# A hybrid S5 and SSD layer: the SSD chain in another order of steps, and C A^j formed a second time instead of stored and loaded

## The chip, the core and the metric

The kernel runs on one core of one Trainium2 chip. Its engines work side by side, each in its own order: TensorE (PE; its weight loads are PEld) multiplies, VectorE (DVE), ScalarE (ACT) and GpSimd (POOL) do elementwise work, and SyncE (SP) issues every DMA of this kernel, one after the other. The metric is the device time of one execution in microseconds; before is the median of three runs.

## What is computed

One layer over 1024 frames of 1024 features: a projection of the normed input feeds two branches, whose outputs are joined by W_out; a gated per-layer input and a last norm follow. The two branches that the change touches, cut to the core:

```python
def s5_branch(u, ...):             # 64 groups of 16 channels, 64 complex states each
    states = A_bar * states_before + u @ B_bar          # per step, a scan
    y = real(states @ C) + D * u
    y = gelu(y); return y * sigmoid(y @ w_glu + b_glu)

def ssd_chunked(xs, dt, A, Bm, Cm):                     # 16 heads, 4 B/C groups, state 128
    xd = xs * dt
    scores = (C @ B.T) * exp(segsum(dt * A))            # decays within a chunk
    y_diag = scores @ xd
    states = B.T @ (decay * xd);  y_off = (C @ states_before) * exp(cumsum(dt * A))
    return y_diag + y_off
```

## The kernel before

A float32 matmul is done as three fast ones: each operand is split in a high and a low part (`whi`, `wlo` from the loaded weights `wraw`), and a dense tile (L163) is 48 matmuls of 512 columns. 56 such tiles run one after the other and make up most of the time: 8 for u, 20 for the convolution and some z (SEQ names them, c or z), 12 more for z, 8 for GLU and 8 for the joint output. In between, generators for the S5 and the SSD branch are moved forward by `pull(gen, n)`, which runs n steps of them; the tables PU, PX, PZ, PG and PO say how many steps follow each tile. The order in which a step is written is only a start: the program is then put in order by a scheduler that simulates time, so an edit in one place can move instructions elsewhere. Each engine runs its own instructions strictly in that order.

S5, with b the eighth of the 64 groups:

- s5_weights (L346 to L399), in the first conv tiles: per b it loads `br` (one buffer, L367) and `gr`, forms `wx` from them (L373 to L376) and the product `CA` = C A^j for nine powers j on VectorE (L386 to L391), stores CA to DRAM as `CAd` (L393), and one b later `strips` multiplies B by CA (L353) and stores the result as `Kd`. `in_line` keeps the strips' matmuls behind the product L374.
- s5_states: loads `ug` (two buffers, L404) and multiplies two b at a time (L428). Then a scan over the states on VectorE (L444, L445).
- s5_out: per b it takes `CAr`, `tp` (cut out of Kd by 8 loads, L473) and ug, all with two buffers and loaded one b ahead (L470), multiplies (L487, L488), applies Gelu on ACT into the buffer of tp, and stores that as `Yd` (L491).

SSD runs over eight k, each 128 frames. Per k: `load` of `cc` (L583) and of `csB` (L586, 1 MB, one row for each head spread over 128 partitions), two buffers each; 16 decays on VectorE (L601) and an exponential on ACT; scores on TensorE (L608), multiplied into csB (L610); xs transposed (L617) and multiplied by dt to `xd` (L621); y on TensorE (L633) with its additions (L635), and from k = 1 on the part from the state (L641, `E0B`); a gate (L648), a norm (L175 to L178, L666) and a store `Sd` (L667); the next state `st` (L675, L680, L682).

## Time and profile before

| | us |
|---|---|
| median of the runs (1004.63 to 1007.05) | 1006.27 |
| the profiled execution | 1008.08 |
| its span, from first to last instruction | 1006.3 |
| PE busy | 964.5 |
| DVE busy | 596.1 |
| ACT busy | 453.3 |
| POOL busy | 215.7 |

The rows of the trace that matter stand in the section on rows. In them L163 is line 163 of the kernel, `out<-in` are the tiles written and read, a number in square brackets is how long the engine stood idle before the instruction and what ended that, and PEclk is the granted clock of TensorE as a share of 2.4 GHz (0.50 is its level of 1.2 GHz).

### The profile page before, as it was taken

The numbers are of one execution on the slowest core, as the hardware profiler recorded it, in microseconds if no ns is written. First come the engines' busy times: TensorE is split into PE (matmuls) and PEld (weight loads), VectorE is DVE, ScalarE is ACT, GpSimd is POOL, SyncE is SP. The second block draws the span as 40 slices with busy tenths as digits, with TensorE's granted clock in tenths as the row PEclk, the third lists the DMA queues.
The fourth block names the chain that finished last, engine by engine and source line by source line (L and its number), as shares of the span: only waits on it lengthen the run. The fifth ranks groups of instructions, "written<-read, shape, count | busy, mean of one in ns | idle before, by whom it ended". The sixth has DMA issues, their size and how long they took to land. (4 is left out here: it accounts for less than half of the span.)

```text
span 1006.3 us, 12839 instructions
## 1 busy us (share of the span) xinstructions
PE 964.5 (96%) x4902; PEld 802.5 (80%) x4902; DVE 596.1 (59%) x959; ACT 453.3 (45%) x583; POOL 215.7 (21%) x150
## 2 busy tenths in 40 slices
PE   9999979997999999989989999899999999999995
PEld 5788857786888888778778888787788888888994
DVE  6599688953988994000656878678611611444436
ACT  7444122354855544224455844557233431463235
POOL 0000000000000043001123445454341284242000
PEclk9999989998999999999989999999999999999998
DMA  7135777568423125997996877465455341010004
GB/s 296 38 88 144 201 221 259 179 191 205 137 94 105 64 105 187 257 261 215 246 310 181 241 188 217 142 168 174 137 167 168 99 128 41 1 67 1 2 1 168
DMA packets 133965, 153.31 MB, mean 152 GB/s; under 512 B 6032, under 2 KB 107408, under 8 KB 132880
## 3 DMA queue, kind: packets, MB, share of 16 engines
q1 hardware_dynamic: 133904, 152.49, 52.0%
q8 instruction: 39, 0.64, 0.3%
q14 instruction: 22, 0.18, 0.1%
HBM read 112.82 MB, written 39.65 MB: 152 GB/s over the span
## 5 line engine op out<-in xcount | busy, mean ns | idle before, releaser
L163 PE MATMUL psd<-xnlo,whi 128*128 128x512 f32 x592 | 185.7, 393 | 0.0
L163 PE MATMUL psd<-xnhi,whi 128*128 128x512 f32 x592 | 185.4, 393 | 0.0
L163 PE MATMUL psd<-xnhi,wlo 128*128 128x512 f32 x592 | 184.3, 392 | 0.2 <-DVE wlo L142 0.2
L139 ACT ACTIVATE whi<-wraw 128x1024 fp32r<-128x1024 f32 x71 | 74.8, 1056 | 217.2 <-PE psd L163 184.7
L142 POOL TENSOR_TENSOR wlo<-wraw,whi 128x1024 fp32r<-128x1024 f32 x44 | 119.2, 2712 | 247.2 <-ACT whi L139 235.8
L163 PEld LDWEIGHTS psd<-xnlo,whi 128*128 128x128 f32 x592 | 110.8, 189 | 24.7 <-issue 1.6
L163 PEld LDWEIGHTS psd<-xnhi,wlo 128*128 128x128 f32 x592 | 110.8, 188 | 24.2 <-issue 1.0
L163 PEld LDWEIGHTS psd<-xnhi,whi 128*128 128x128 f32 x592 | 111.0, 189 | 23.1 <-issue 0.4
L601 DVE SCALAR_TENSOR_TENSOR csB<-csB,csM,cst_t 128x128 f32<-128x128 f32 x128 | 45.9, 432 | 101.3 <-DMA m<-Yd 94.0
L574 DVE SCALAR_TENSOR_TENSOR cv<-pad,prm_t,cv 128x1024 f32<-128x1024 f32 x48 | 65.7, 1369 | 12.1 <-ACT cv L572 11.9
L565 POOL MEMSET pad<- 128x3 f32 x16 | 1.6, 103 | 215.8 <-DMA Cd<-pad 169.6
L892 DVE TENSOR_TENSOR h<-h,psd 128x512 f32<-128x512 f32 x16 | 10.4, 684 | 63.3 <-PE psd L163 63.3
L163 PE MATMUL psd<-hhi,wlo 128*128 128x384 f32 (+2 forms) x168 | 46.9, 340 | 0.0
L163 PE MATMUL psd<-hlo,whi 128*128 128x384 f32 (+2 forms) x168 | 46.7, 338 | 0.0
L163 PE MATMUL psd<-hhi,whi 128*128 128x384 f32 (+2 forms) x168 | 46.5, 338 | 0.0
L933 DVE TENSOR_TENSOR gt<-psd,rstdB 128x384 f32<-128x384 f32 (+2 forms) x21 | 11.1, 559 | 52.3 <-PE psd L163 42.3
L142 DVE TENSOR_TENSOR wlo<-wraw,whi 128x1024 fp32r<-128x1024 f32 x27 | 32.9, 1220 | 14.3 <-ACT whi L139 14.3
L163 PE MATMUL psd<-yhi,whi 128*128 128x512 f32 x128 | 41.0, 398 | 0.0
L163 PE MATMUL psd<-yhi,wlo 128*128 128x512 f32 x128 | 40.7, 395 | 0.0
L163 PE MATMUL psd<-mhi,wlo 128*128 128x512 f32 x128 | 40.0, 391 | 0.0
L163 PE MATMUL psd<-ylo,whi 128*128 128x512 f32 x128 | 40.0, 391 | 0.0
L163 PE MATMUL psd<-mlo,whi 128*128 128x512 f32 x128 | 39.5, 390 | 0.0
(292 smaller groups left out, 1878.0 us busy)
## 6 DMA issues: line engine op xcount, KB each, us to landing
wraw<-in_w_in_dram SPq DMA_DIRECT2D x39, 512.0 KB, 3.7
Cd<-pad SPq DMA_DIRECT2D x16, 512.0 KB, 3.1
Zd<-z SPq DMA_DIRECT2D x16, 512.0 KB, 3.8
ug<-Ud SPq DMA_DIRECT2D x16, 512.0 KB, 6.6
cc<-Cd SPq DMA_DIRECT2D x8, 1024.0 KB, 9.0
csB<-Rd SPq DMA_DIRECT2D x8, 1024.0 KB
wraw<-in_w_out_dram SPq DMA_DIRECT2D x16, 512.0 KB, 4.3
CAd<-CA SPq DMA_DIRECT2D x16, 288.0 KB, 4.6
```

The source lines that it names most:

```text
L139: S.activation(hi, raw, AF.Copy)
L142: E.tensor_tensor(lo, raw, f(hi), ALU.subtract)
L163: T.matmul(p, w[:, c], rhs[k][r][:, x], start=(k == 0 and j == 0), stop=(k == nk - 1 and j == 2))
L565: G.memset(pad[:, 8:11, 0:1], 0.0)
L574: conv_last[0] = V.scalar_tensor_tensor(cv, pad[:, d:d + 8, 1:129], pr("convw", 4 * m + d), cv, ALU.mult, ALU.add)
L601: i_ = V.scalar_tensor_tensor(csB[:, h], csB[:, h], csM[:, 16 * k + h:16 * k + h + 1], cap, ALU.subtract, ALU.min)
L892: V.tensor_tensor(hf(h_t[m], h), hf(h_t[m], h), ps[h], ALU.add)
L933: first = V.tensor_tensor(gt, pg[i], rstdB[:, c], ALU.mult)
```

## The change

S5's weights. CA has eight powers instead of nine, its store CAd goes, the strips are no longer held behind L374, and the first two entries of PX are 1 and 5 instead of 3 and 3.

```diff
-PX = [3, 3, 1, 1, 2, 1, 2, 1, 0, 2, 1, 2, 2, 0, 1, 1, 2, 2, 2, 2]
+PX = [1, 5, 1, 1, 2, 1, 2, 1, 0, 2, 1, 2, 2, 0, 1, 1, 2, 2, 2, 2]
...
-            def strips(b, CA, behind):
+            def strips(b, CA):
                 kp = psa()
                 for q in range(4):
                     for ri in range(2):
-                        i_ = T.matmul(kp[32 * q:32 * q + 32, 0:P], Bbd[:, ri, 4 * b + q, :],
-                                      CA[:, ri, q, 0:8, :].rearrange("p a b -> p (a b)"),
-                                      start=(ri == 0), stop=(ri == 1), tile_position=(0, 32 * q))
-                        in_line((behind, i_))
+                        T.matmul(kp[32 * q:32 * q + 32, 0:P], Bbd[:, ri, 4 * b + q, :],
+                                 CA[:, ri, q].rearrange("p a b -> p (a b)"),
+                                 start=(ri == 0), stop=(ri == 1), tile_position=(0, 32 * q))
...
-                behind = V.tensor_tensor(w1, br, gr[:, 1:2].broadcast_to([P, 2, 512]), ALU.mult)
+                V.tensor_tensor(w1, br, gr[:, 1:2].broadcast_to([P, 2, 512]), ALU.mult)
...
-                CA = q2.tile([P, 2, 4, 9, 16], F32, tag="CA", name="CA")
-                ca1 = q2.tile([P, 4, 9, 16], F32, tag="ca1", name="ca1", bufs=1)
+                CA = q2.tile([P, 2, 4, 8, 16], F32, tag="CA", name="CA")
+                ca1 = q2.tile([P, 4, 8, 16], F32, tag="ca1", name="ca1", bufs=1)
...
-                er = Er[:, J0:J0 + 9, g4].rearrange("p j g -> p g j")[:, :, :, None].broadcast_to(sh)
+                er = Er[:, J0:J0 + 8, g4].rearrange("p j g -> p g j")[:, :, :, None].broadcast_to(sh)
...
-                for g2 in range(2):
-                    dma(CAd[b, g2].rearrange("r n c -> n r c"),
-                        CA[64 * g2:64 * g2 + 64].rearrange("p a b c d -> p a (b c d)"))
                 if b > 0:
-                    strips(b - 1, last, behind)
+                    strips(b - 1, last)
                 last = CA
                 yield
-            strips(7, last, behind)
+            strips(7, last)
```

S5's output. CAr is not loaded; a new input `crow` holds C with the states along the rows, of which `cb` (128 KB) is loaded for each b. `EO` holds the powers, copied once by ACT in eight pieces of 64x256. `rows(b)` forms C A^j again in three VectorE operations of 128x1024, one b ahead. The old body of s5_out did the same matmuls with CAr in place of CA.

```diff
     def load_out(q4, b):
-        CA = q4.tile([P, 2, 4, 144], F32, tag="CAr", name="CAr")
-        dma(CA.rearrange("p a b c -> p a (b c)"), CAd[b].rearrange("g r n c -> (r n) g c"))
+        cb = q4.tile([P, 2, 8, 16], F32, tag="cb", name="cb")
+        dma(cb, crow[:, b])
         tp = q4.tile([P, 8, P], F32, tag="tp", name="tp")
         for s in range(8):
             dma(tp[16 * s:16 * s + 16],
                 Kd[b].rearrange("(g h) c -> h g c", h=16)[:, :, 112 - 16 * s:240 - 16 * s])
-        return CA, tp, load_u(q4, b)
...
+        return cb, tp, load_u(q4, b)
+
+    def s5_out(Er, Ei, wx, q4, ahead):
+        with tc.tile_pool(name="q5", bufs=1, side="right") as q5:
+
+            EO = q5.tile([P, 2, 8, 64], F32, tag="EO", name="EO")
+            lo_, up = slice(0, 64), slice(64, P)
+            for g2, src in enumerate((lo_, up)):
+                for r, j, x, sign in ((lo_, 0, Er, 1.0), (lo_, 1, Ei, 1.0), (up, 0, Ei, -1.0), (up, 1, Er, 1.0)):
+                    S.activation(EO[r, j, :, g2:64:2], x[src, J0 + 1:J0 + 9], AF.Copy, scale=sign)
+
+            def rows(b, cb):
+
+                CA = q5.tile([P, 8, 8, 16], F32, tag="CAo", name="CAo", bufs=2)
+                t = q5.tile([P, 8, 8, 16], F32, tag="cat", name="cat")
+                for j, dst in ((0, CA), (1, t)):
+                    V.tensor_tensor(dst, cb[:, j, :, None, :].broadcast_to([P, 8, 8, 16]),
+                                    EO[:, j, :, 8 * b:8 * b + 8].rearrange("p j g -> p g j")[:, :, :, None].broadcast_to([P, 8, 8, 16]),
+                                    ALU.mult)
+                V.tensor_tensor(CA.rearrange("p g j c -> p (g j c)"), CA.rearrange("p g j c -> p (g j c)"),
+                                t.rearrange("p g j c -> p (g j c)"), ALU.subtract)
+                return CA
+            CA = rows(0, ahead[0][0])
             yield
+            for b in range(8):
+                _, tp, ug = ahead.pop(0)
+                if b < 7:
+                    ahead.append(load_out(q4, b + 1))
+                    nxt = rows(b + 1, ahead[0][0])
+                ysb = tp.rearrange("p (q g) c -> p q g c", g=2)
+                for g2 in range(2):
+                    yp = psa()
+                    for q in range(4):
+                        o = yp[:, q * P:(q + 1) * P]
+                        g = 2 * q + g2
+                        T.matmul(o, tp[:, g, :], ug[:, g, :], start=True, stop=False)
+                        T.matmul(o, CA[:, g].rearrange("p j c -> p (j c)"), wx[:, 8 * b + g].rearrange("p r c -> p (r c)"), start=False, stop=True)
+
+                    S.activation(ysb[:, :, g2, :].rearrange("p q (s j) -> p q s j", j=8), js(yp), AF.Gelu_apprx_tanh)
+                dma(Yd[8 * b:8 * b + 8].rearrange("g t h c -> (t h) g c"), tp)
+                CA = nxt
+                yield
```

SSD. csB is loaded ahead of cc and both two k ahead; the decays of k + 1 are made in two halves in iteration k, its scores and the load E0B at the end of iteration k; two more steps are pulled before the loop.

```diff
                 cc = p4.tile([P, 16, P], F32, tag="cc", name="cc", bufs=2)
-                dma(cc, Cd[:, :, k * P:(k + 1) * P].rearrange("m p c -> p m c"))
                 csB = p4.tile([P, 16, P], F32, tag="csB", name="csB", bufs=2)
                 src = Rd[0, 16 * k:16 * k + 16, :].rearrange("h l -> (h l)")
                 dma(csB.rearrange("p h l -> p (h l)"), src[None].broadcast_to([P, 2048]))
+                dma(cc, Cd[:, :, k * P:(k + 1) * P].rearrange("m p c -> p m c"))
                 return cc, csB
...
+            def load_e(k):
+
+                E0B = p4.tile([P, 8, P], F32, tag="E0B", name="E0B", bufs=1)
+                for hh in range(2):
+                    dma(E0B[64 * hh:64 * hh + 64], Rd[1, 16 * k + hh:16 * k + 16:2, :][None].broadcast_to([64, 8, P]))
+                return E0B
+
+            def decays(k, csB, half):
+                for h in range(8 * half, 8 * half + 8):
                     i_ = V.scalar_tensor_tensor(csB[:, h], csB[:, h], csM[:, 16 * k + h:16 * k + h + 1], cap,
-                                           ALU.subtract, ALU.min)
+                                                ALU.subtract, ALU.min)
                     if k == 0:
                         in_line((conv_last[0], i_))
-                S.activation(csB, csB, AF.Exp)
+                if half:
+                    S.activation(csB, csB, AF.Exp)
+
+            def scores(cc, csB):
                 sp = psa()
                 for g in range(4):
                     T.matmul(sp[:, g * P:(g + 1) * P], cc[:, 8 + g], cc[:, 12 + g], start=True, stop=True)
                 for g in range(4):
                     V.tensor_tensor(csB[:, 4 * g:4 * g + 4], csB[:, 4 * g:4 * g + 4],
                                     sp[:, None, g * P:(g + 1) * P].broadcast_to([P, 4, P]), ALU.mult)
+
+            st = None
+            cur, nxt = load(0), load(1)
+            yield
+            for half in range(2):
+                decays(0, cur[1], half)
+            yield
+            scores(*cur)
+            yield
+            for k in range(8):
+                cc, csB = cur
+                zc = p4.tile([P, 8, P], F32, tag="zc", name="zc")
+                dma(zc, Zd[8:16, :, k * P:(k + 1) * P].rearrange("m p c -> p m c"))
                 xd = p4.tile([P, 16, 64], F32, tag="xd", name="xd")
                 xd2 = p4.tile([P, 16, 64], F32, tag="xd2", name="xd2") if k < 7 else None
...
                 yield
-                if k < 7:
-                    nxt = load(k + 1)
...
+                if k < 7:
+                    decays(k + 1, nxt[1], 0)
                 yield
...
+                    decays(k + 1, nxt[1], 1)
                 yield
...
                     st = st2
+                    E0B = load_e(k + 1)
+                    scores(*nxt)
+                    cur = nxt
+                    nxt = load(k + 2) if k < 6 else None
                 yield
...
+    cn = lambda c: c.transpose(2, 0, 1).reshape(64, 8, 8, 16)
+    a["crow"] = np.ascontiguousarray(np.tile(np.stack([cn(one["s5_C_re"]), cn(one["s5_C_im"])], 2), (2, 1, 1, 1, 1)))
```

Line numbers of the new program differ: there L371, L372 and L374 are the wx of before, L384 to L389 make CA, L468 loads tp, L486 and L489 are `rows`, L509 stores Yd, L618 are decays, L630 scores, L654 xd, L666 the additions to ys, L681 the gate, L700 the norm's product and L716 copies of st.

On VectorE, in the strips of b = 1 and 2, before (ca_851 and ca_852 are the halves of CA(2), which the third group of strips reads):

```order
L388 TENSOR_TENSOR CA<-ca_851,ca_852 128x576
L373 TENSOR_TENSOR wx<-br,gr 128x1024
L374 TENSOR_TENSOR w_843<-br,gr 128x1024
L389 TENSOR_TENSOR ca_851<-csb,Ei 128x576
L390 TENSOR_TENSOR ca_852<-csb,Er 128x576
L142 TENSOR_TENSOR wlo<-wraw,whi 128x1024
L376 TENSOR_TENSOR wx<-wx,w_843 128x8x64 x2
L574 SCALAR_TENSOR_TENSOR cv<-pad,prm_t,cv 128x1024
L391 SCALAR_TENSOR_TENSOR CA<-ca_851,ca_852 128x576
```

and now, where ca_846 and ca_847 are those halves:

```order
L386 TENSOR_TENSOR CA<-ca_846,ca_847 128x512
L357 SCALAR_TENSOR_TENSOR Ks<-cst_t,prm_t,psa 128x16
L358 COPY Ks<-psa 128x112
L374 TENSOR_TENSOR wx<-wx,w_806 128x8x64 x2
L387 TENSOR_TENSOR ca_846<-csb,Ei 128x512
L388 TENSOR_TENSOR ca_847<-csb,Er 128x512
L371 TENSOR_TENSOR wx<-br,gr 128x1024
L372 TENSOR_TENSOR w_838<-br,gr 128x1024
L389 SCALAR_TENSOR_TENSOR CA<-ca_846,ca_847 128x512
```

The last operation of CA(2) stood behind wlo, two sums of wx and a conv step (L574), and now stands right behind the products wx.

On SP, in the output stage, from the load of ug(3) on, before:

```order
L404 DMA ug<-Ud 128x8x128
L470 DMA CAr<-CAd 128x2x576
L491 DMA Yd<-tp 128x8x128
L473 DMA tp<-Kd 16x8x128 x8
L808 DMA Zd<-z 128x1024
L473 DMA tp<-Kd 16x8x128 x8
L138 DMA wraw<-in_w_in_dram 128x1024
L404 DMA ug<-Ud 128x8x128
L470 DMA CAr<-CAd 128x2x576
L491 DMA Yd<-tp 128x8x128
L404 DMA ug<-Ud 128x8x128
```

and now, from the store of b = 1 on:

```order
L509 DMA Yd<-tp 128x8x128
L468 DMA tp<-Kd 16x8x128 x16
L465 DMA cb<-in_crow_dram 128x256
L846 DMA Zd<-z 128x1024
L137 DMA wraw<-in_w_in_dram 128x1024
L399 DMA ug<-Ud 128x8x128
L509 DMA Yd<-tp 128x8x128
L465 DMA cb<-in_crow_dram 128x256
L399 DMA ug<-Ud 128x8x128
L468 DMA tp<-Kd 16x8x128 x8
L509 DMA Yd<-tp 128x8x128
```

Before, the stores of b = 2 and 3 were both issued ahead of the loads of tp(4); now the loads of tp(4), eight of them, stand between Yd(2) and Yd(3), and so on for the following b.

On VectorE, in SSD, from the scores of k = 0 on (xd_3875 belongs to k = 1), before:

```order
L610 TENSOR_TENSOR csB<-csB,psa 128x512 x4
L601 SCALAR_TENSOR_TENSOR csB<-csB,csM,cst_t 128x128 x16
L635 SCALAR_TENSOR_TENSOR ys<-cc,prm_t,psa 128x128 x8
L648 TENSOR_TENSOR ys<-ys,zc 128x1024
L176 TENSOR_TENSOR nl<-zc,nh 128x512
L682 COPY st<-psa 128x512 x2
L666 TENSOR_TENSOR ys<-ys,zc 128x1024
L610 TENSOR_TENSOR csB<-csB,psa 128x512 x4
L601 SCALAR_TENSOR_TENSOR csB<-csB,csM,cst_t 128x128 x11
L621 TENSOR_TENSOR xd<-psa,dt_76 128x512
L621 TENSOR_TENSOR xd_3875<-psa,dtd 128x512
```

and now, from the decays of k = 0 on:

```order
L618 SCALAR_TENSOR_TENSOR csB<-csB,csM,cst_t 128x128 x32
L630 TENSOR_TENSOR csB<-csB,psa 128x512 x4
L654 TENSOR_TENSOR xd<-psa,dt_76 128x512
L654 TENSOR_TENSOR xd_3745<-psa,dtd 128x512
L654 TENSOR_TENSOR xd<-psa,dt_76 128x512
L654 TENSOR_TENSOR xd_3745<-psa,dtd 128x512
L666 SCALAR_TENSOR_TENSOR ys<-cc,prm_t,psa 128x128 x8
L681 TENSOR_TENSOR ys<-ys,zc 128x1024
L175 TENSOR_TENSOR nl<-zc,nh 128x512
L618 SCALAR_TENSOR_TENSOR csB<-csB,csM,cst_t 128x128 x16
L716 COPY st<-psa 128x512
L700 TENSOR_TENSOR ys<-ys,zc 128x1024
```

32 decays, those of k = 0 and 1, now stand ahead of the scores of k = 0, and the 16 decays of k = 2 ahead of the copies of st, the norm's product and, behind those, the scores (L630) and xd of k = 1; before, 11 decays of k = 2 stood behind the scores of k = 1 and ahead of its xd.

## Rows read from the trace of the kernel before

**Rows 1.** Page, busy us (share of the span) and number of instructions of each engine.

```profile
PE 964.5 (96%) x4902; PEld 802.5 (80%) x4902; DVE 596.1 (59%) x959; ACT 453.3 (45%) x583; POOL 215.7 (21%) x150
```

**Rows 2.** Waits of TensorE: tile, line, for what: us in total, times, longest.

```profile
PE psa L353 <- DVE CA L391: 7.5, 1, 7.5
PE psa L428 <- DMA ug<-Ud: 5.5, 1, 5.5
PE psa L487 <- DMA tp<-Kd: 5.2, 3, 2.8
...
PE psa L617 <- ACT zc L663: 2.1, 1, 2.1
```

**Rows 3.** Timeline of TensorE, SSD's y: start us, us, ..., xcount, [idle before <-releaser].

```profile
489.90 3.21 PE L633 MATMUL psa<-csB,xd 128*64 128x128 f32 x32 [1.72 <-DVE csB L610]
...
523.20 1.97 PE L633 MATMUL psa<-csB,xd 128*64 128x128 f32 x16 [3.59 <-DVE xd L621]
```

**Rows 4.** Stretches behind two waits: engines' busy us (xinstructions), then PEclk, DMA share, GB/s.

```profile
142.70:146.10 3.40, 3.40 (x20) 2.52 (x21) 3.40 (x5) 0.00 (x0) 0.00 (x0) 0.50 1.01 284
...
519.61:528.90 9.29, 5.70 (x40) 4.93 (x40) 8.36 (x25) 3.23 (x3) 1.01 (x2) 0.63 1.00 337
```

**Rows 5.** Timeline of TensorE, dense matmuls ahead of the strips' wait.

```profile
129.91 0.61 PE L163 MATMUL psd<-xnhi,whi 128*128 128x512 f32 x2
...
131.72 0.62 PE L163 MATMUL psd<-xnlo,whi 128*128 128x512 f32 x2
```

**Rows 6.** Timeline of VectorE, the products wx and the last operation of CA(2).

```profile
124.89 1.23 DVE L373 TENSOR_TENSOR wx<-br,gr 128x1024 f32<-128x1024 f32 x1 [1.87 <-DMA br<-in_brow_dram]
...
134.71 1.23 DVE L373 TENSOR_TENSOR wx<-br,gr 128x1024 f32<-128x1024 f32 x1 [3.93 <-DMA br<-in_brow_dram]
...
141.86 0.75 DVE L391 SCALAR_TENSOR_TENSOR CA<-ca,ca 128x576 f32<-128x576 f32 x1
```

**Rows 7.** Timeline of SP, issues of br in the strips.

```profile
118.70 0.38 SPq L367 DMA_DIRECT2D br<-in_brow_dram  x1
...
127.28 0.39 SPq L367 DMA_DIRECT2D br<-in_brow_dram  x1
```

**Rows 8.** Timeline of SP, issues of ug in the states (the first with ug(1)).

```profile
213.67 2.09 SPq L404 DMA_DIRECT2D ug<-Ud  x2
...
226.98 0.38 SPq L404 DMA_DIRECT2D ug<-Ud  x1
```

**Rows 9.** Stretch of the output stage, columns as in rows 4.

```profile
395.00:476.00 81.00, 75.85 (x424) 66.14 (x423) 0.00 (x0) 27.04 (x35) 11.96 (x5) 0.98 0.89 247
```

**Rows 10.** Instructions of tile wlo on POOL: ns min/median/max, first and last start us.

```profile
L142 POOL TENSOR_TENSOR wlo<-wraw,whi x44: 2360/2402/7515, 360.9 to 922.7; 128x1024 fp32r<-128x1024 f32 x44
```

**Rows 11.** Timeline of SP, store of b = 0 and loads of b = 2 and 3.

```profile
392.68 0.68 SPq L491 DMA_DIRECT2D Yd<-tp  x1
...
401.21 5.67 SPq L473 DMA_DIRECT2D tp<-Kd  x8
```

**Rows 12.** Timeline of TensorE, first and last output matmuls.

```profile
388.54 0.39 PE L488 MATMUL psa<-wx,CAr 128*128 128x128 f32 x2
...
463.19 0.39 PE L488 MATMUL psa<-wx,CAr 128*128 128x128 f32 x2
```

**Rows 13.** Timeline of SP, loads csB of k = 1 and k = 2.

```profile
480.64 4.30 SPq L586 DMA_DIRECT2D csB<-Rd  x1
...
509.97 0.74 SPq L586 DMA_DIRECT2D csB<-Rd  x1
```

**Rows 14.** Timeline of VectorE in SSD, k = 0 and 1.

```profile
493.31 4.29 DVE L601 SCALAR_TENSOR_TENSOR csB<-csB,csM,cst_t 128x128 f32<-128x128 f32 x16 [1.68 <-DMA csB<-Rd]
...
513.59 2.48 DVE L610 TENSOR_TENSOR csB<-csB,psa 128x512 f32<-128x512 f32 x4
518.90 3.64 DVE L601 SCALAR_TENSOR_TENSOR csB<-csB,csM,cst_t 128x128 f32<-128x128 f32 x11 [2.83 <-DMA csB<-Rd]
522.47 0.68 DVE L621 TENSOR_TENSOR xd<-psa,dt 128x512 f32<-128x512 f32 x1
```

More of the change, by code (lines that the diff above doesn't have):

```diff
@@ L60, in hybrid_layer @@
 def hybrid_layer(ctx: ExitStack, tc: tile.TileContext, xT, pT, w_in, w_dt, w_glu, w_out, w_gate, w_ple,
-                 prm, cst, bst, cstt, brow, out):
+                 prm, cst, bst, cstt, crow, brow, out):
     nc = tc.nc
@@ L474, in load_out @@
                 Kd[b].rearrange("(g h) c -> h g c", h=16)[:, :, 112 - 16 * s:240 - 16 * s])
-        return CA, tp, load_u(q4, b)
-    def s5_out(wx, q4, ahead):
-        for b in range(8):
-            CA, tp, ug = ahead.pop(0)
-            if b < 7:
-                ahead.append(load_out(q4, b + 1))
-            ysb = tp.rearrange("p (q g) c -> p q g c", g=2)
-            for g2 in range(2):
-                yp = psa()
-                for q in range(4):
-                    o = yp[:, q * P:(q + 1) * P]
-                    T.matmul(o, tp[:, 2 * q + g2, :], ug[:, 2 * q + g2, :], start=True, stop=False)
-                    T.matmul(o, CA[:, g2, q, 16:144], wx[:, 8 * b + 2 * q + g2].rearrange("p r c -> p (r c)"), start=False, stop=True)
-                S.activation(ysb[:, :, g2, :].rearrange("p q (s j) -> p q s j", j=8), js(yp), AF.Gelu_apprx_tanh)
-            dma(Yd[8 * b:8 * b + 8].rearrange("g t h c -> (t h) g c"), tp)
-            yield
+        return cb, tp, load_u(q4, b)
@@ L506, in s5_chain @@
         yield from s5_states(Er, Ei, wx, q4, ahead)
-        yield from s5_out(wx, q4, ahead)
+        yield from s5_out(Er, Ei, wx, q4, ahead)
         es_s.close()
```

21 lines of the change are left out of this document (4 added, 17 removed).

## The prediction

> **What bounds the kernel now.** I read the page's busy times first: TensorE is busy 964.5 of 1006.3 us, 96 % [rows 1]. The change leaves the matmuls as they are (3702 dense ones in either program, and the same strips, state, output and SSD ones), so it can win only the time in which TensorE stands still or runs at half clock. The waits of TensorE come next [rows 2]: 7.5 us in S5's strips for the product CA, 5.5 us in S5's states for the load ug, 5.2 us in three waits of S5's output for tp, and 2.1 us in SSD for a transpose whose buffer ACT has not emptied. Two more stand in the timeline of TensorE [rows 3]: SSD's y of k = 0 waited 1.72 us, that of k = 1 3.59 us. Behind the long waits the granted clock is low: 0.50 over the 3.4 us that follow the strips' wait, 0.63 from the wait of y(1) to the end of what follows it [rows 4]. Half clock over 3.4 us costs 1.7 us, and I put 1.7 to 2.5 us behind each of the strips, the states, the last output wait and the two y. Some 26 us of waits and 10 us of half clock are all that can be won in the middle of this kernel. What stands behind each wait is the queue of SP, which issues every load in one order, or VectorE, which does its work in one order; so I read those two around each wait.
>
> **The unit.** Eight dense matmuls take 131.72 − 129.91 = 1.81 us, 0.226 us each [rows 5]. Distances on TensorE below are counts of dense matmuls between two places in the order of each program, times this.
>
> **S5's strips.** CA loses a ninth of its columns (128x512 for 128x576), 48 operations save about 0.08 us each (0.75 × 64/576 [rows 6]), and 16 stores go from SP. The strips come nearer: the last seven matmuls of strips(2) have 463 dense matmuls before them instead of 482, which is 19 × 0.226 = 4.3 us earlier. strips(2) waited 7.5 us, from 135.2 to 142.7, for CA(2) [rows 2], whose last operation ran at 141.86, behind the products wx [rows 6]. Those need the load br, which has one buffer: br is issued when the second product of the b before has ended, at 118.70 and 127.28 [rows 7], and its first reader starts at 124.89 and 134.71 [rows 6], 6.2 and 7.4 us later. In the new order CA(2) ends right behind these two products, without wlo and a conv step (1.1 + 1.2 us) between. With the stores gone from the same queue I take 5.5 us for a br load (bounds: 5 and 7.4 us). Product of b1 at 123.7, its second ended at 126.0, br(2) there at 131.6, two products and the last CA operation 3.0 us more: 134.6. TensorE is at strips(2) at about 135.2 − 4.3 + 1.6 (what strips(1), now 42 dense matmuls earlier, waits for CA(1)) = 132.5. That leaves 1.6 + 2.1 = 3.7 us of waits and about 1 us of half clock where 7.5 and 1.9 were: **+4.7 us** (bounds −1 and +9).
>
> **S5's states.** The second pair waits for ug(2), issued at 226.98, 13.3 us behind ug(0) at 213.67 [rows 8]. Two CAr loads (1.15 MB) leave the stretch between, two cb loads of 128 KB come in. At the 247 GB/s of the nearest loaded stretch [rows 9] the 0.9 MB less are 3.6 us. But the second pair has come nearer to the first as well, 24 dense matmuls instead of 36, 2.7 us. The third pair stands 23 behind it as before, but runs into its own load sooner, since the second no longer runs at half clock. I take 3.5 us of waits and 2 us of half clock against 5.5 and 2.4: **+2.3 us** (−3 and +5).
>
> **Rows formed on VectorE.** The 24 new 128x1024 operations are of the kind of the wx product, 1.23 us each [rows 6], 29 us in all. Their place had VectorE idle: 0.00 us busy from 395 to 476 [rows 9]. So 21 of them cost nothing as long as they stay under the spacing of the outputs (3.7 us for one b, formed one b ahead, against 3.2 us of output matmuls and 2 us or more of dense ones). The first three and the eight copies of EO on ACT stand between the last scan operation and the first output; in the order 37 dense matmuls' worth of other work covers most of that. **−1 us** (0 and −3). Beside them on POOL run the subtractions that make wlo, 2.40 us as a rule, but 7.5 us at the longest [rows 10], and that one ran while VectorE scanned. The Trainium skill (SBUF — State Buffer, Who interferes with whom) says that VectorE and GpSimd share one port pair, which one operation holds until its end, when VectorE reads two inputs from SBUF. The 7.5 us agree with that, and by the rule the new operations would meet seven wlo's at 2.4 us each, 17 us that the idle 81 us of VectorE hold; it speaks against the first three operations alone, which could come 2.4 us later.
>
> **S5's output: the queue order.** tp(b+2) takes the buffer of tp(b), so its 8 loads wait for the store Yd(b). Before, Yd(0) was issued at 392.68 and the first load of tp(2) at 401.21, 8.5 us later; the 8 loads took 5.7 us to issue [rows 11]. Before, the stores went two at a time ahead of the loads, so two b shared one such trip. Now, from b = 4 on, the loads of tp(4) stand ahead of Yd(3) in SP's queue, tp(5) ahead of Yd(4), tp(6) ahead of Yd(5): four trips in a row. With CAr gone (576 KB against 128 KB for each b) I take 6 us for a trip and 4.5 us for the 8 issues, 10.5 us in all (bounds 4.5 + 3.8 = 8.3 and 8.5 + 5.4 = 13.9). Yd(0) goes out 4.1 us behind the first output matmul (392.68 − 388.54), tp(2) is there 10.5 us later and some 2.4 us to land (an estimate), at 17.0, and Yd(2) follows 4.1 us behind that and 0.4 us of queue, at 21.5 us. Four trips later, 2.4 us to land and 3.2 us of matmuls more, the stage ends: 21.5 + 42 + 5.6 = 69.1 us. Before it lasted from 388.54 to 463.58, 75.0 us [rows 12]; with the 31 dense matmuls that now stand behind it taken off (7.0 us) 68.0. So −1.1 us, and about 2 us more of half clock, since three waits of 2 to 5 us stand where three of at most 2.8 us were [rows 2]: **−3 us** (−18 and +8).
>
> **SSD, y(0).** y(0) stands 137 dense matmuls behind the last output instead of 100, 8.4 us of cover: TensorE comes at 488.2 + 8.4 = 496.6 in the times of before. VectorE now does 32 decays, of k = 0 and 1, ahead of the scores of k = 0. The second half needs csB(1), issued before at 480.64 [rows 13] and read from 493.31 [rows 14]. Ahead of it in the queue 1.5 MB less are asked for: 6.1 us earlier, 487.2. Then 4.29 us of decays, 2.48 us of scores and two xd (1.2 us) [rows 14]: 495.2. The 1.72 us and the half clock behind them go, but for 0.4 us: **+3.0 us** (−5 and +3.4).
>
> **SSD, y(1).** Before, csB(2) was issued at 509.97 [rows 13], 20.1 us behind the start of y(0) at 489.90 [rows 3]; its first decay began at 518.90, xd followed 11 decays later at 522.47 [rows 14] and y(1) at 523.20. The scores of k = 1 ran while csB(2) was under way. Now all 16 decays of k = 2 stand **ahead** of these scores and of xd(1). From csB(2) on: 4.29 + two copies and a product (2.4) + scores 2.48 + two xd 1.2 = 10.4 us to y(1). TensorE comes 29.7 + 0.7 (three dense matmuls more) − 1.7 (no half clock) = 28.7 us behind y(0). csB(2) has 1 MB more ahead of it, but y(0) starts 8 us later behind the output: 26.5 us behind y(0) if the queue paces it, 20 us if traffic is light; I take 24.3, so y(1) at 34.7 and a wait of 6.0 instead of 3.59 us: **−2.4 us** (−6 and +5).
>
> **Rest of SSD.** Scores and transposes of the same k now stand half a tile apart, so the transposes find an emptied buffer: the 2.1 us [rows 2]; decays of k+2 stand ahead of the norm in both programs. **+2.1 us** (−3 and +4).
>
> **Sum.** 4.7 + 2.3 − 1 − 3 + 3.0 − 2.4 + 2.1 = 5.7 us. The profiled execution took 1008.08 us (span 1006.3 and 1.8 around it), 0.2 % above the median of 1006.27; the difference goes off the median: **1000.6 us**.
>
> **Rivals.** *All cover holds* (0.17): a trip takes 8.3 us and csB(2) lands 20 us behind y(0). The output ends at 59.6 (+8.4), y(1) waits 1.7 us with no half clock behind (+4.7 with the 2.8 us of that), nothing is late behind the scan: 25 us, 981 us. For it: the loads that go were the largest in that stretch; against it: the 512 KB of ug, Zd and weights stay. *The output's queue order decides* (0.17), on the other side: with trips of 13.9 us as before, and Yd(2) 3 us later for the same reason, the stage ends at 24.5 + 55.6 + 5.6 = 85.7 us, −17.7 us and 2 us of clock: 1017 us. It turns the whole slower from 11.9 us a trip on (4 × 11.9 + 27.1 = 74.7 = 68.0 + the 8.7 us of the other terms − 2 us of clock). For it: 8.5 and 5.7 us are this trace's own; against it: they were measured with CAr on the queue. *The waits move along with TensorE* (0.13): br and ug land as late against their readers as before, since one buffer and one queue pace them, and the two S5 terms go: 1007.6 us. *The port* (0.06): the first rows meet a wlo and come 2.4 us later, and half clock follows: 1003.5 us. The Trainium skill's page named above is the rule for this one.
>
> **Chances.** My forecast has 0.42, and 0.05 is left for what I have not seen. About 0.3 % (3 us) can be told from no change, so the bounds are 1003.2 and 1009.3. Faster: 0.33 of the forecast's 0.42, 0.17, 0.03 of the moved waits, 0.02 of the port and 0.02 of the unseen, 0.57. Same: 0.08, 0.08 of the moved waits, 0.04 of the port, 0.03 of the slow trips, 0.23. Slower: the rest, 0.20. The range of 984 to 1013 leaves out the best of the first rival and the worst of the second.
>
> **What would show it.** In the trace of after: the wait of strips(2) for CA near 2 us; that of the states for ug near 3; VectorE busy some 30 us in the output stage with no output waiting for CAo; waits for tp at b = 5 and 7 of 3 to 5 us, and Yd(3) issued behind the 8 loads of tp(4); y(0) without a wait and y(1) waiting 4 to 8 us for xd, with decays of csB(2) just before. I am wrong if a trip in the output is under 9 or over 11.9 us, if csB(2) lands before TensorE has done the transposes of k = 1, or if the strips still wait 7 us.

## The result and the profile after

The median went from 1005.45 us (1004.22 to 1007.05) to 994.64 us (993.96 to 998.64), a ratio of 0.9905 with an interval of 0.9883 to 0.9927: 10.8 us faster where 5.7 were forecast. The profiled execution of after took 993.96 us (span 992.1), 14.1 us less than that of before; the terms below are set against these 14.1.

The page answers rows 1 (busy us, share, instructions):

```profile
PE 959.4 (97%) x4902; PEld 796.8 (80%) x4902; DVE 629.2 (63%) x983; ACT 449.5 (45%) x586; POOL 212.0 (21%) x150
```

TensorE has the same 4902 instructions and is busy 5.1 us less, at a higher granted clock (0.988 over the whole span, 0.982 before). The waits of TensorE answer rows 2 (tile, line, for what: us in total, times, longest):

```profile
PE psa L176 <- ACT nh L174: 5.4, 1, 5.4
PE psa L505 <- DMA tp<-Kd: 5.0, 3, 2.0
PE psa L352 <- DVE CA L389: 3.3, 2, 2.3
...
PE psa L423 <- DMA ug<-Ud: 2.5, 1, 2.5
PE psa L177 <- DVE nl L175: 1.2, 1, 1.2
```

The strips (L352) and the states (L423) wait less than half as long as in rows 2, the output about as long. Both y of rows 3 (L664 now) run without a wait, as does the rest of the SSD, where 5.1 us were. But the largest wait of all is new: the norm of k = 0 (L176). Here it is in TensorE's timeline (start us, us, what, [idle before <-releaser]), the first matmuls of y(1) behind it:

```profile
498.41 0.80 PE L176 MATMUL psa<-nh,ones_r 128*128 128x512 f32 x1 [5.38 <-ACT nh L174]
...
500.88 0.79 PE L177 MATMUL psa<-nl,ones_r 128*128 128x512 f32 x1 [1.24 <-DVE nl L175]
...
518.49 1.09 PE L664 MATMUL psa<-csB,xd 128*64 128x128 f32 x16
```

ACT, at the same place:

```profile
485.77 1.06 ACT L682 ACTIVATE zc<-ys 128x1024 f32<-128x1024 f32 x1 [1.20 <-DVE ys L681]
496.79 1.06 ACT L138 ACTIVATE whi<-wraw 128x1024 fp32r<-128x1024 f32 x1 [9.95 <-DMA wraw<-in_w_in_dram]
497.75 0.61 ACT L174 ACTIVATE nh<-zc 128x512 fp32r<-128x512 f32 x1
```

And SP, which issued the wraw that ACT waited for:

```profile
477.37 10.16 SPq L874 DMA_DIRECT2D m<-Yd  x7
...
489.24 0.84 SPq L137 DMA_DIRECT2D wraw<-in_w_in_dram  x1
...
491.18 0.40 SPq L605 DMA_DIRECT2D csB<-Rd  x1
```

Read from the bottom: SP spends 10.16 us on seven loads of m, GLU's input, which nobody reads before 545.6 us. Behind them comes wraw; its split whi is next in ACT's order, and nh stands behind whi, though what nh itself needs, a sum made by GpSimd, was ready at 488.19 us. TensorE stands 5.38 us for a copy of 0.61 us that waits for someone else's load. csB(2) is behind the same m loads. The stretches of rows 4 are now these (columns as there):

```profile
135.40:138.00 2.60, 2.60 (x23) 2.06 (x24) 2.60 (x4) 0.00 (x0) 0.09 (x1) 1.00 0.71 230
...
220.80:224.20 3.40, 3.37 (x17) 3.40 (x18) 2.37 (x2) 0.59 (x1) 0.00 (x0) 0.56 1.10 378
496.90:507.10 10.20, 7.45 (x20) 5.68 (x21) 7.70 (x19) 7.75 (x10) 2.36 (x1) 0.50 1.01 347
```

Behind the strips' 2.26 us no half clock follows; behind the states' 2.50 us 3.4 us of it; around the norm's wait 10.2 us, in which TensorE was busy for 7.45 us, some 3.7 us longer than at full clock.

### The profile page after: what moved, and what is told of

Its sections match the earlier page's. It is cut to its first block, busy times and chain, and to the rows that moved or that the text cites. A ratio compares the mean times of both kernels' runs of the same rounds, so it can differ in the third digit from the quotient of the medians.

```text
span 992.1 us, 12846 instructions
## 1 busy us (share of the span) xinstructions
PE 959.4 (97%) x4902; PEld 796.8 (80%) x4902; DVE 629.2 (63%) x983; ACT 449.5 (45%) x586; POOL 212.0 (21%) x150
## 4 chain that ended last, share of the span: by engine, by line
PE 74%; DMA 8%; DVE 7%; SPq 6%; issue 2%; ACT 2%; DVEq 0%; POOL 0%; ACTq 0%; POOLq 0%
PE psd L162 61%; SPq L874 2%; SPq L468 2%; DMA Yd<-tp 2%; PE psa L162 2%; PE psa L672 2%; PE psa L664 1%; PE psa L709 1%; DMA tp<-Kd 1%; PE psa L423 1%; DMA br<-in_brow_dram 1%; PE psa L505 1%; DVE xnlo L812 1%; DMA wraw<-in_w_in_dram 1%; PE psa L506 1%
## 5 line engine op out<-in xcount | busy, mean ns | idle before, releaser
L141 POOL TENSOR_TENSOR wlo<-wraw,whi 128x1024 fp32r<-128x1024 f32 x44 | 113.0, 2572 | 237.2 <-ACT whi L138 230.5
L162 PEld LDWEIGHTS psd<-xnhi,wlo 128*128 128x128 f32 x592 | 110.7, 188 | 24.3 <-issue 1.0
L618 DVE SCALAR_TENSOR_TENSOR csB<-csB,csM,cst_t 128x128 f32<-128x128 f32 x128 | 50.4, 466 | 38.4 <-DMA csB<-Rd 38.4
L162 PE MATMUL psd<-mhi,whi 128*128 128x512 f32 x128 | 39.5, 390 | 0.0
L162 PE MATMUL psd<-nhi,wlo 128*128 128x512 f32 x128 | 39.4, 389 | 0.0
```

Of the source, the lines that this page charges most:

```text
L141: E.tensor_tensor(lo, raw, f(hi), ALU.subtract)
L162: T.matmul(p, w[:, c], rhs[k][r][:, x], start=(k == 0 and j == 0), stop=(k == nk - 1 and j == 2))
L618: i_ = V.scalar_tensor_tensor(csB[:, h], csB[:, h], csM[:, 16 * k + h:16 * k + h + 1], cap, ALU.subtract, ALU.min)
```

## The experiments

For all kernels one table: idle time of TensorE (stretches over 0.06 us) in the profiled execution, added by stage, and the time at half clock between the first strips and the tail. (The stages are stretches of time; 2.0 of the 11.7 us in the SSD of ssd_only are at dense tiles.) A single execution strays by some us: that of s5_only took 989.26 us, 5.6 under its median. How far the waits stray shows where kernels run the same order. ssd_only has the order of before on every engine up to 460 us, and waits 4.8 and 3.5 us in strips and states where before waits 7.5 and 5.5. Eight kernels (after, s5_only, nh_pool, mhold, mhold_nl, tp3, combo, s5_mhold) have one order through the strips, and wait 1.4 to 4.4 us there. Each ratio is against runs of before from the same group, whose medians were 1005.45 us (after), 1003.46 (s5_only, ssd_only, nh_pool, mhold), 1004.25 (inline, cad_store, mhold_nl, tp3) and 1005.21 (the others); so kernels of different groups are compared by ratio.

| | strips | states | output | SSD | half clock | median us | ratio (95 %) |
|---|---|---|---|---|---|---|---|
| before | 7.5 | 5.5 | 5.2 | 10.4 | 27.3 | 1005.45 | |
| after | 3.3 | 2.5 | 5.0 | 6.6 | 13.7 | 994.64 | 0.9905 (0.9883–0.9927) |
| s5_only | 1.4 | 2.5 | 4.4 | 9.1 | 6.8 | 994.84 | 0.9913 (0.9886–0.9941) |
| ssd_only | 4.8 | 3.5 | 4.2 | 11.7 | 23.9 | 1005.61 | 1.0021 (0.9998–1.0044) |
| inline | 2.3 | 2.8 | 3.9 | 9.7 | 20.5 | 997.07 | 0.9928 (0.9891–0.9965) |
| cad_store | 2.4 | 2.3 | 5.1 | 9.3 | 17.1 | 995.16 | 0.9898 (0.9869–0.9927) |
| nh_pool | 3.7 | 2.4 | 4.1 | 5.5 | 13.7 | 991.94 | 0.9892 (0.9859–0.9924) |
| mhold | 3.8 | 2.3 | 4.7 | 3.7 | 3.4 | 987.37 | 0.9853 (0.9819–0.9888) |
| mhold_nl | 1.7 | 2.5 | 3.3 | 0.7 | 3.4 | 983.30 | 0.9782 (0.9753–0.9812) |
| tp3 | 3.2 | 1.9 | 6.5 | 0.0 | 6.8 | 988.58 | 0.9826 (0.9786–0.9866) |
| combo | 4.3 | 2.1 | 6.3 | 0.7 | 6.8 | 988.50 | 0.9829 (0.9785–0.9873) |
| combo_br | 43.3 | 3.3 | 2.0 | 0.0 | 58.0 | 1028.30 | 1.0233 (1.0193–1.0273) |
| s5_mhold | 4.4 | 1.5 | 3.2 | 9.8 | 13.7 | 994.90 | 0.9898 (0.9853–0.9943) |
| before_mhold | 7.4 | 5.0 | 5.0 | 12.8 | 17.1 | 1008.08 | 1.0037 (1.0007–1.0067) |

### The two halves

**s5_only**: the change of S5, with the SSD chain as before.

```diff
-            cur, nxt = load(0), load(1)
+            nxt = load(0)
...
-                if k < 7:
-                    decays(k + 1, nxt[1], 0)
```

> The S5 half of the change alone (CA of eight powers, no CAd, rows formed again for the output), SSD as before. Theory from the two traces: the S5 stages carry the gain by themselves; strips, states and output gave back 7.50 + 5.45 + 5.16 us of waits against 3.25 + 2.50 + 4.97 now, and some 5.8 us of half clock against 1.5: 11 to 12 us, less what the old SSD order still waits at its y. So 994 to 996 us, with y(0) and y(1) waiting 1.5 to 4 us as before. Rival: the halves need each other, since an earlier S5 meets SSD's old order with the same loads on the queue; then 1000 to 1003 us and longer waits at y(0) and y(1).

**ssd_only**: the change of the SSD chain, with S5 as before.

```diff
-        cb = q4.tile([P, 2, 8, 16], F32, tag="cb", name="cb")
-        dma(cb, crow[:, b])
+        CA = q4.tile([P, 2, 4, 144], F32, tag="CAr", name="CAr")
+        dma(CA.rearrange("p a b c -> p a (b c)"), CAd[b].rearrange("g r n c -> (r n) g c"))
```

> The SSD half alone, S5 as before. Theory: y(0) and y(1) no longer wait and the later SSD waits (5.1 us in all before) go, 3.4 + 6.4 + 5.1 us, but the norm of k = 0 waits for its high part on ACT as in the whole change (5.4 + 1.2 us and 3.7 us of half clock): 4 to 5 us faster, 1000 to 1002 us, strips and states waiting 7.5 and 5.5 us as before. Rival: the wait at the norm comes only from the earlier end of S5, so it is not there and the time is 990 to 994 us.

S5's half alone gives 0.9913 and the whole change 0.9905, which the intervals don't tell apart; the SSD's half alone gives 1.0021, whose interval holds 1. The time of s5_only came as its theory had it, though y(1) waits longer than the 1.5 to 4 us. Of ssd_only neither expectation came: nothing is gained, and the norm of k = 0 waits 0.5 us. In each half the wait stands at another instruction; TensorE of s5_only, then of ssd_only:

```profile
506.63 1.97 PE L652 MATMUL psa<-csB,xd 128*64 128x128 f32 x16 [6.42 <-DVE xd L640]
```

```profile
514.21 1.11 PE L631 MATMUL psa<-cst_t,cc 128*128 128x128 f32 x4 [6.75 <-DVE st L697]
```

y(1) waits 6.42 us in the old order, where TensorE comes sooner than before. The new order moves this to the transposes here and to the norm in after. The copy of st that these transposes wait for stands on VectorE of ssd_only behind 11 decays, and those waited for csB(2):

```profile
510.58 2.98 DVE L599 SCALAR_TENSOR_TENSOR csB<-csB,csM,cst_t 128x128 f32<-128x128 f32 x11 [10.83 <-DMA csB<-Rd]
```

So the pipeline as it stands won nothing that these runs show, and moved a wait.

### The strips: order on VectorE or traffic of the stores

**inline**: after with the strips held behind the second product of wx again.

```diff
+                        in_line((behind, i_))
...
-                V.tensor_tensor(w1, br, gr[:, 1:2].broadcast_to([P, 2, 512]), ALU.mult)
+                behind = V.tensor_tensor(w1, br, gr[:, 1:2].broadcast_to([P, 2, 512]), ALU.mult)
```

> The changed kernel with one removed line put back: the strips of b - 1 are again kept behind the second wx product of b. The groups of strips then stand where they stood before (427 dense matmuls ahead of the third group, against 391 and 415), all else of the change stays. Theory A (what shortened the strips' wait is that CA comes sooner: no stores on the queue and the CA operation right behind the wx products): TensorE comes later to the same CA(2), the strips wait 0 to 1 us, and the time is that of the changed kernel or 2 us less. Theory B (the earlier strips are what gained, by pulling the states forward): 2 to 4 us slower than the changed kernel.

**cad_store**: after with the 16 stores of CA (eight powers) put back, which nothing reads.

```diff
+                for g2 in range(2):
+                    dma(CAd[b, g2].rearrange("r n c -> n r c"),
+                        CA[64 * g2:64 * g2 + 64].rearrange("p a b c d -> p a (b c d)"))
```

> The changed kernel with the 16 stores of CA put back (256 KB each, to memory that nothing reads), so the traffic and the places on SP's queue that they cost come back, while C A^j is still formed a second time. Theory A (traffic): the wx product of b = 2 starts 2 to 3 us later, the strips wait 5 to 6 us with half clock behind, the states wait 1 to 2 us longer: 998 to 1000 us. Theory B (the order on VectorE alone shortened the strips' wait): waits as in the changed kernel, 994 to 996 us.

Neither brings the 7.5 us back: the strips wait 2.3 and 2.4 us. With the stores on the queue the first wx product of b = 2, which waits for br, starts at 131.64 us, in after at 132.38. So nothing shows that the stores hold br up, and cad_store came as its theory B had it. What these three kernels share, and before has not, is the place of CA(2)'s last operation on VectorE. After:

```profile
132.38 1.23 DVE L371 TENSOR_TENSOR wx<-br,gr 128x1024 f32<-128x1024 f32 x1 [1.53 <-DMA br<-in_brow_dram]
133.53 1.22 DVE L372 TENSOR_TENSOR w<-br,gr 128x1024 f32<-128x1024 f32 x1
134.66 0.69 DVE L389 SCALAR_TENSOR_TENSOR CA<-ca,ca 128x512 f32<-128x512 f32 x1
```

It runs 2.28 us behind the start of the first product, in before 7.15 us [rows 6]; with the stores it ran at 130.44 us, ahead of that product. That the order is the cause is what remains of the listed edits, not a test of its own: no run changed only that order. Its size is uncertain too: the three kernels with the order of before wait 7.5, 4.8 (ssd_only) and 7.4 us (before_mhold) in the strips. The time of inline, 997.07 us, lies in the range of its theory B, but its interval overlaps that of after, and the states, on which theory B rests, wait hardly longer (2.8 us for 2.5). inline loses in the SSD instead: the norm waits 8.5 us in it.

### The norm: whose queue

**nh_pool**: nh of k = 0 copied by POOL, so that it no longer stands behind whi on ACT.

```diff
-        S.activation(hi, v, AF.Copy)
+        if pool:
+            G.tensor_copy(hi, v)
+        else:
+            S.activation(hi, v, AF.Copy)
```

> The changed kernel with one instruction on another engine: the high part nh of the norm of k = 0 is copied by POOL instead of ACT, so it no longer stands behind the split of late weights on ACT. Theory A: the wait of 5.4 us at that norm, the 1.2 us behind it and the half clock (3.7 us) go and nothing takes their place: 984 to 986 us. Theory B, the one of the prediction's step on y(1): the decays of k = 2, which stand ahead of the scores of k = 1, then set y(1): csB(2) is read from 501.8, y(1) can start about 513, and TensorE would be there about 508: a wait of 4 to 6 us and half clock there, 990 to 993 us.

The norm no longer waits, and the next reader of ACT's queue does, the state's product with BT, whose copy stands behind the same whi (TensorE, then ACT):

```profile
499.79 1.22 PE L712 MATMUL psa<-xd,BT 128*128 128x256 f32 x2 [5.46 <-ACT BT L694]
```

```profile
497.24 1.06 ACT L138 ACTIVATE whi<-wraw 128x1024 fp32r<-128x1024 f32 x1 [10.46 <-DMA wraw<-in_w_in_dram]
498.20 1.07 ACT L208 ACTIVATE z<-psd 128x512 f32<-128x512 f32 x2
499.15 0.59 ACT L694 COPY BT<-psa 128x512 f32<-128x512 f32 x1
```

A wait that goes at one line and comes at the next, behind the same release, says that the blocked queue is the cause, not the copy. The time, 991.94 us, lies in the range of theory B, but y(1) does not wait: the number came by another instruction.

**mhold**: the loads of m held behind the store of the z tile two before, so they reach SP's queue later and a few at a time.

```diff
-        dma(Zd[m], z)
+        zd.append(dma(Zd[m], z))
...
+                in_line((zd[-2], i_))
```

> The changed kernel with the 16 loads of m (256 KB each) held on SP's queue behind the store of the z tile two before, one pair for each tile, so that weights and csB(2) do not queue behind eleven of them. Theory A (the queue of SP and its traffic make both the weights behind which nh stands and csB(2) late): no wait at the norm of k = 0, csB(2) there some 8 us sooner, no wait at y(1): 984 to 986 us. Theory B (the wait at the norm comes from the order on ACT alone): it stays above 3 us, 992 to 995 us.

About 5 us less than after by the ratios (0.9853 and 0.9905), whose intervals just touch. Theory A came in its main part: the wraw whose split stands ahead of nh goes out at 474.77 us (489.24 in after), the split runs at 484.90 without a wait for it, and nh is in time.

```profile
474.77 2.72 SPq L137 DMA_DIRECT2D wraw<-in_w_in_dram  x1
```

The load itself was no faster (it landed 9.4 us after its issue; in after its split began 7.5 us after it): it was issued sooner. What is left, and keeps the time above the 984 to 986 us of theory A, is a smaller wait, on VectorE:

```profile
492.44 4.29 DVE L618 SCALAR_TENSOR_TENSOR csB<-csB,csM,cst_t 128x128 f32<-128x128 f32 x16 [10.25 <-DMA csB<-Rd]
496.65 0.68 DVE L175 TENSOR_TENSOR nl<-zc,nh 128x512 fp32r<-128x512 f32 x1
```

VectorE stood 10.25 us for csB(2), with nl(0), the low part for the norm, behind 16 decays; TensorE waited 3.72 us for it. In after the scheduler had put nl(0) ahead of these decays; here it put it behind them.

**mhold_nl**: mhold, and the decays of k + 2 issued behind nl of k.

```diff
+                    if k - 2 in nl_k:
+                        in_line((nl_k[k - 2], i_))
```

> The kernel with the loads of m held, and one order more on VectorE: the decays of k + 2 stand behind the norm's low part nl of k. In the run with m held alone TensorE waited 3.72 us for nl of k = 0, which stood behind 16 decays that waited for csB(2). Theory A (each wait of VectorE for csB is handed to whatever stands behind it): the 3.72 us and the 1.7 us of half clock go, y(1) then waits 0 to 2 us: 982 to 984 us on the scale of the run with m held (987.4). Theory B (the wait moves on to y(1), since the scores of k = 1 still stand behind the decays of k = 2): y(1) waits 3 to 4 us, 986 to 988 us.

983.30 us, 0.9782: the lowest time of the study, 2.2 % under before, and as theory A had it. Two waits of 0.4 and 0.3 us are all that is left in its SSD:

```profile
PE psa L178 <- ACT nh L176: 0.4, 1, 0.4
...
PE psa L179 <- DVE nl L177: 0.3, 1, 0.3
```

**s5_mhold**: the loads held in the same way, S5 changed, the SSD chain as before (s5_only with mhold's edit).

```diff
+                in_line((zd[-2], i_))
```

> S5 with C A^j formed a second time, the SSD chain in its old order, and the m loads held as above. What is the pipeline of the SSD worth by itself once the loads no longer come late? Theory (the old order still puts the decays and scores of the next chunk behind the y products, so that y(1) waits): a wait of 4 to 6 us at y(1) stays with its stretch of half clock, 988 to 990 us, against 983.3 us of the pipeline with the same held loads and its decays in place. Rival (y(1) waited only because whi's split was late): no wait there over 1.5 us, 985 us or less, and the pipeline is worth nothing by itself.

Neither expectation came in. The 6.42 us at y(1) are gone, but not the time: 994.9 us, and 9.8 us of SSD waits in ten pieces, for nh, nl, csB, st and xd:

```profile
PE psa L176 <- ACT nh L174: 3.0, 3, 1.9
PE psa L177 <- DVE nl L175: 2.8, 3, 1.1
...
PE psa L652 <- DVE csB L629: 1.6, 1, 1.6
PE psa L636 <- DVE st L699: 1.2, 1, 1.2
```

Against mhold_nl (0.9898 to 0.9782, intervals apart) the pipeline with nl ahead of the decays is worth about 1 % once SP brings its loads in time; against mhold alone (0.9853) the intervals overlap. And the held loads by themselves won nothing that shows in the old order: 0.9913 in s5_only, 0.9898 here.

**before_mhold**: the kernel before with the loads of m held.

```diff
+                in_line((zd[-2], i_))
```

> The kernel before with one edit: the m loads held behind the store of an earlier z tile. Theory (the same queue of loads on SP caused the waits of 1.72 and 3.59 us at y(0) and y(1) in the kernel before): these 5.3 us and what of the clock went with them go, 997 to 1000 us. Rival (those waits came from the order of the SSD chain itself): no change, 1003 to 1006 us.

A trifle slower (1.0037), with 12.8 us of SSD waits for 10.4, so the theory fell. The queue of m was not what the kernel before waited for in its SSD; the wait for wraw behind m came with the change, which brings TensorE to the SSD 10.4 us sooner (y(0) at 479.47 us, 489.90 in rows 3).

### The output's buffers

**tp3**: three buffers of tp.

```diff
-        tp = q4.tile([P, 8, P], F32, tag="tp", name="tp")
+        tp = q4.tile([P, 8, P], F32, tag="tp", name="tp", bufs=3)
```

> The changed kernel with three buffers for tp instead of two, so that the loads of tp(b+2) wait for the store of b - 1 and no longer for that of b. Theory (the output stage is paced by the trips from store to load): the three waits for tp (1.0, 1.9, 2.0 us) go, and the stage from the first to the last output matmul takes 60 to 62 us instead of 65.9: 4 to 5 us faster than the changed kernel, 989 to 990 us. Rival (the traffic of ug, tp, Zd and weights paces it, not the order): at least 3 us of waits stay, 993 to 995 us; or the 5 us come back as a wait in SSD, whose loads share the queue.

0.9826, a gain, and near the time of the theory, but not where a third buffer would show: the waits of the output rose from 5.0 to 6.5 us, for tp, cb and ug (1.1 us without a releaser). The stage lasts 53.5 us instead of 65.9, since the scheduler puts fewer dense matmuls between its outputs and more behind them; the long row of m loads goes out at 460.79 (eight in 10.59 us) instead of 477.37 us, and no SSD instruction waits. The gain shows in the SSD.

**combo**: mhold_nl and tp3 together.

```diff
+                    if k - 2 in nl_k:
+                        in_line((nl_k[k - 2], i_))
...
-        tp = q4.tile([P, 8, P], F32, tag="tp", name="tp")
+        tp = q4.tile([P, 8, P], F32, tag="tp", name="tp", bufs=3)
...
+                in_line((zd[-2], i_))
```

> The changed kernel with three edits together: the m loads held behind the store of an earlier z tile, the decays of the next chunk issued behind nl(k) on VectorE, and tp in three buffers instead of two. Theory (the waits of the output stage come from tp's two buffers, and are independent of the SSD waits): the run with tp alone had 6.5 us of waits left in an output stage of 53.5 us, the run with the first two edits had 983.3 us and no wait in the SSD; together 978 to 981 us, no wait over 1 us in the SSD. Rival (tp's three buffers already end S5 early enough that the loads of m no longer matter, and the 6 us of output waits stay): about 983 us, no better than the first two edits without tp. Rival 2 (ended earlier, the SSD's loads meet other transfers and a wait comes back): 986 us or more, with a wait of 3 us or more in the SSD.

My theory fell: 988.5 us. The SSD is as free as in mhold_nl, and the output waits 6.3 us as in tp3 (3.3 in mhold_nl). The two edits win the same thing by two ways; the third buffer adds output waits on top. The 5 us of the medians are more than those 3. The strips' 4.3 us, against 1.7, are no work of the edits: both kernels have one order there, and other executions of it waited as long. The intervals of the two ratios overlap, so that combo is slower than mhold_nl isn't settled.

**combo_br**: combo with two buffers of br.

```diff
-                br = q2.tile([P, 2, 512], F32, tag="br", name="br", bufs=1)
+                br = q2.tile([P, 2, 512], F32, tag="br", name="br")
```

> The kernel of combo with br in two buffers in place of three, which moves the loads of br and of the states far earlier or later in the dense order. Theory (waits of the strips and states come from where their loads stand in SP's queue, and this order starts them sooner): 2 to 4 us of waits less at strips and states than in combo, so about 3 us faster. Rival (the moved loads and states only meet other queues): no gain, within 2 us of combo, or slower with a wait of 4 us or more at the strips, whose br buffer comes free later.

The text has the buffers wrong: br had one and got two, not three and two. Neither expectation has a loss of this size: the kernel is 2.3 % slower than before. SP's waits from 120 to 190 us (line <- whom: us in total, times, longest):

```profile
SPq L361 <- DVE Ks L360: 34.3, 6, 11.1
SPq L367 <- DVE w L374: 21.4, 5, 10.0
```

and VectorE's over the same time:

```profile
DVE wx L373 <- DMA gr<-Gd: 15.5, 6, 4.6
```

With br free the scheduler drew the strips together (TensorE is busy 19.2 of 61.0 us from 135 to 196). The store of a strip (L361) then waits on SP for TensorE and VectorE, and the loads of br and gr behind it are what VectorE needs for the next strip: a ring of three engines, with half clock for 51.2 us. So a buffer more took away the cover that had hidden SP's order; this is read from one trace, and no run undid it.

## Why the prediction came out as it did

Five of the seven terms had the right sign; the rows cost nothing, and the output gained where a loss was forecast. The sum of 5.7 us is short of the 14.1 us of the profiled execution (10.8 by the medians), and that it is no further off owes something to terms that missed in both directions. The terms, with half clock counted as in the prediction:

| term | forecast | trace of after |
|---|---|---|
| strips | +4.7 | +6.1 |
| states | +2.3 | +3.9 |
| rows on VectorE | −1 | 0 |
| output | −3 | +1.7 |
| y(0) | +3.0 | +3.4 |
| y(1), with the norm ahead of it | −2.4 | −3.9 |
| rest of SSD | +2.1 | +5.1 |
| head and a wait at 767 us, not forecast | 0 | −1.8 |

Together 14.5 us, against 14.1. Not all of this is the change: the profiled execution of before was a long one (1008.08 us against a median of 1005.45), and in ssd_only the same order waited 2.7 and 2.0 us less in strips and states.

- **Strips: near in the times, wrong in a reason.** CA(2)'s last operation was to end at 134.6 us and ended at 135.35. A br load took 6.6 us from issue (125.76) to its reader (132.38), not 5.5; TensorE came at 133.1, not 132.5. That the missing stores speed br up fell with cad_store; the order on VectorE, the other half of the step, is what remains. What was over-forecast is half clock: 2.26 us of waiting were followed by none. The two changed entries of PX move nothing: with 3 and 3 the ordered program is the same on every engine but for the numbers in some names; no run was made of it.
- **States.** One wait of 2.50 us and 3.4 us at half clock, where 3.5 us of waiting and 2 us lost to half clock were forecast.
- **Rows.** The output never waited for CAo. The 24 operations took 1.22 us each, 29 us in all, as forecast. One wlo of POOL did run in among the first rows:

```profile
374.20 2.73 POOL L141 TENSOR_TENSOR wlo<-wraw,whi 128x1024 fp32r<-128x1024 f32 x1 [5.34 <-ACT whi L138]
...
373.45 1.22 DVE L486 TENSOR_TENSOR cat<-cb,EO 128x1024 f32<-128x1024 f32 x1
374.58 3.42 DVE L593 SCALAR_TENSOR_TENSOR cv<-pad,prm_t,cv 128x1024 f32<-128x1024 f32 x1
377.93 1.21 DVE L489 TENSOR_TENSOR CAo<-CAo,cat 128x1024 f32<-128x1024 f32 x1
```

  A conv step beside it (wlo from 374.20 to 376.93) took 3.42 us instead of 1.3. CAo(0) was ready at 379.14, the first output ran at 380.74: 1.6 us of cover were left.
- **Output: the queue order right, the trip too long.** SP's timeline has the order that was forecast, each store behind the eight loads of the b after:

```profile
403.14 0.37 SPq L509 DMA_DIRECT2D Yd<-tp  x1
...
408.67 3.64 SPq L468 DMA_DIRECT2D tp<-Kd  x8
412.40 0.38 SPq L509 DMA_DIRECT2D Yd<-tp  x1
...
415.84 4.75 SPq L468 DMA_DIRECT2D tp<-Kd  x8
...
421.63 0.53 SPq L509 DMA_DIRECT2D Yd<-tp  x1
```

  From store to store 9.3, 9.2, 10.2 (to 431.79) and 9.4 us (to 441.18), not 10.5: four trips took 38.0 us, not 42. So the stage lasts 65.9 us (380.74 to 446.61), not 69.1, though Yd(2) came 22.4 us behind the first output and not 21.5. Waits of 1.0, 1.9 and 2.0 us (b = 2, 5 and 7) came in place of 3 to 5, and no half clock followed them. The rival of slow trips, from 11.9 us on, is out, and so is that of the cover that holds everywhere, which needed trips of 8.3 us. The waits did not move along with TensorE: strips and states waited less. The port did not delay the first output.
  Two figures of these rivals don't come out of the step's own terms: with trips of 8.3 us the stage ends at 58.1 and not 59.6, and the whole turns slower from 11.6 and not 11.9 us a trip, since the first trip lies ahead of Yd(2) and moves it too. With trips of 9.2 to 10.2 us neither matters.
- **y(0).** No wait, no half clock, as forecast but for 0.4 us.
- **y(1): a loss of about the forecast size came, by luck, at another instruction.** y(1) was put 34.7 us behind y(0), paced by xd(1) and csB(2). VectorE of after shows that it was not:

```profile
501.83 4.29 DVE L618 SCALAR_TENSOR_TENSOR csB<-csB,csM,cst_t 128x128 f32<-128x128 f32 x16 [1.00 <-DMA csB<-Rd]
...
512.70 0.69 DVE L654 TENSOR_TENSOR xd<-psa,dt 128x512 f32<-128x512 f32 x1 [1.87 <-PE psa L650]
```

  The first operation of xd(1) ended 33.9 us behind y(0) (513.39), but it had waited 1.87 us for the transposes (L650) of TensorE, which the norm had made late. csB(2) was there 22.4 us behind y(0), not 24.3. In nh_pool, where VectorE does not wait between csB(2) and xd(1), these took 9.6 us (502.21 to 511.82), not 10.4. That puts y(1) at 32.0 us. TensorE was put 28.7 us behind; it came at 39.0, less 5.38 and 1.24 of waits and 3.7 of half clock, 28.7. So y(1) would have waited some 3.3 us (an estimate from these rows), not 6.0, had the norm not waited 6.6 us ahead of it; no run shows that wait. One of the prediction's own signs of being wrong came with it: csB(2) was there at 501.83 us, and TensorE did the transposes of k = 1 from 512.07 on. The step that failed is the reading of one queue only: csB(2) was followed through SP and VectorE, while wraw, behind the same m loads on SP, was not followed to whi on ACT and nh behind it. With the 3.7 us at half clock this cost 1.5 us more than forecast.
- **Rest of SSD.** 2.1 us were counted, the one wait of rows 2; the other 3.0 us of small waits went too. Behind y(1), s5_mhold in the old order has 5.7 us of such waits; in the new order after has none, mhold_nl 0.7, and ssd_only 2.5 (and 2.0 at dense tiles). So most of that part is the pipeline's.

## What to carry to other kernels

Follow a late load through every engine that reads from the same stretch of SP's queue: here the wait appeared at the first instruction that TensorE met behind a blocked engine, and when that was taken away, at the next. Mend such a chain at its head (hold loads that nobody needs for 50 us), not at the line that waits, and only where TensorE waits for it: the same hold won nothing in before_mhold and s5_mhold. The pipeline of the SSD's steps paid only when its loads and the short operations that TensorE needs stood ahead of the work it brings forward. A buffer more let the scheduler move everything around it, so its effect is to be read from the whole trace. And before a wait of 3 us is explained, see how much it differs between executions of one order.
